# Four gate chunks move from the attention filler to a sixth Strassen group of the projections

## The chip, the cores and the metric

The kernel runs on one core of one Trainium2 chip. The metric is the device time of one execution in microseconds; the median of several runs is compared.

## What is computed

One layer of a bidirectional encoder: 1024 tokens of width 1024, all in float32. The reference, cut to what matters here:

```python
h = x + 0.5 * swiglu(rms_norm(x, n1), ...)            # feed-forward, d_ff = 2816
u = rms_norm(h, nm)
z = u @ w_in                                          # 1024 x 4352, one combined projection
qa, ka, va, qb, kb, vb, ga, gb = split(z)             # 3 x 512, 512, 2 x 128, 1024, 1024 columns
ya = neighbourhood_attention_2d(qa, ka, va, rpb)      # branch A: 8 heads of 64
yb = windowed_gqa_sink(rope(qb), rope(kb), vb, sink)  # branch B: 8 heads, 2 key/value heads
merged = sigmoid(ga) * (ya @ w_branch_a) + sigmoid(gb) * (yb @ w_branch_b)
h = h + merged @ w_out
h = h + 0.5 * swiglu(rms_norm(h, n2), ...)
y = rms_norm(h, nf)
```

## The kernel before, in words

Every large product is taken in three terms of 32-bit "high" and "low" parts: an operand is copied to a rounded high part (ScalarE) and the rest is subtracted out as a low part (VectorE, in places GpSimd), and `mm3` (L145, L147, L149) issues high x high, high x low and low x high, each a matmul with 128 x 512 output.

The order on every engine after the first stage is made by a planner: it takes the program in the order in which Python traced it as a priority, has costs of its own for each instruction, and issues what is ready by those costs. The order on each engine is then fixed. PSUM has two pools of four banks, called "d" and "g" in the names of the tiles.

The stages, in order of time, are: the first feed-forward (Strassen products, first its up, then its down part); the projections; attention, in which other products fill TensorE; the branch products; the product with `w_out`; and the second feed-forward.

**Projections.** The 34 chunks of 128 columns of `w_in` are numbered 0 to 33: 0 to 17 are queries, keys and values; 18 to 25 are the gates `ga` and 26 to 33 the gates `gb`. The list `groups` (L875) names chunks that are taken four at a time as a Strassen group: seven products (P1 to P7) for each of two pairs, `products` (L233 on) makes their operands (L308 on ScalarE, L311 and L315 on VectorE), and `store_z` (L879) evicts them and writes them to DRAM by GpSimd's queue. Hooks (L1030 on) place rotations, loads and reorderings of the other steps at fixed places before the end of this stage, and those at its start move with the number of groups.

**Attention.** `units_b` and then `units_a` give 64 units, 32 for each branch. For a unit, `scores` (L1278, L1279) issues the matmuls of two heads into two "d" banks, VectorE adds bias and takes the maximum (L1283), ScalarE takes the exponential (L1286), VectorE the reciprocal (L1289), and both engines scale (L1290, L1291). `turn` transposes on TensorE (L1299) into two "d" banks and splits the result into high and low parts (L93, L94). `values` (L1313 or L1318) multiplies with the values into a "g" bank, and `write` adds the parts (L1252 to L1256 for branch A). In one round of the loop the scores of unit n, the turn of unit n-1 and the values of unit n-2 are traced.

**The filler.** Between these steps the loop pulls steps of six large matmuls (two banks, three terms) from a generator, `filler`:

- first a `gate` for each gate chunk that is in no group: eight steps; its weights are split 1024 columns wide (L93, L94), its two "g" banks are copied out by ScalarE (L1127), and a DMA writes them to `g_d` (L1128);
- then `branch_b`: eight chunks of four steps, `yb @ w_branch_b`. Each splits a weight of 512 columns, loads a chunk of `gb` from `g_d` into one of two "xs" buffers (L1178), takes its sigmoid on ScalarE (L1179), and multiplies two banks, "d" for even chunks and "g" for odd ones, with it on VectorE (L1197);
- last, three of four steps of two chunks of `ya @ w_branch_a` (`branch_a`).

How many steps are pulled for a unit is set by `rate`; what is left is drained right after the loop. Before the change the 14 gates have 112 steps, `nfill` is 150 and `rate` is 106/64.

After that the branch-A products run chunk by chunk with sigmoids of `ga` (L1393), and GpSimd's queue stores combinations for the `w_out` product, which is a Strassen product again (`Down`).

Of the kernel before, what the change touches and what calls it, by code (L numbers as in the profile page):

```python
# [36 lines left out]
def trunk_kernel(ctx, tc, x, xt, n1, wg1, wu1, wd1, nm, win, rpb, sink, wa, wb, wo,  # L37
# [834 lines left out]
    mix = {}  # L872


    groups = [[(12, 13), (14, 15)], [(16, 17), (0, 1)], [(4, 5), (8, 9)], [(2, 3), (6, 7)], [(10, 11), (18, 19)]]  # L875
    NG = len(groups)
    gates = [dc for dc in [*range(8, 16), *range(8)] if 18 + dc not in sum((p for g in groups for p in g), ())]

# [336 lines left out]
    nfill = len(gates) * 8 + 38  # L1215
# [103 lines left out]
        un["write"](o)  # L1319

    pipe = []
    rate = (nfill - 44) / 64.0
    spent = 3.0

    def filling(share):
# [231 lines left out]
```

## Time and profile before

| quantity | before |
|---|---|
| median of 3 runs | 1936.27 us (1935.07 to 1936.42) |
| profiled execution: span | 1934.8 us |
| profiled execution: its own time | not listed apart; its span lies 0.3 us below the fastest run |
| TensorE busy | 1922.2 us (99%) |
| VectorE busy | 1437.1 us (74%) |
| ScalarE busy | 943.6 us (49%) |
| GpSimd busy | 295.5 us (15%) |

In the rows of the profile PE is TensorE's matmuls, PEld its weight loads, DVE is VectorE, ACT ScalarE, POOL GpSimd, and SP the engine that issues most loads. A row of a stretch gives its start and end, its length, the busy time of each engine in it with the number of instructions, TensorE's granted clock and the share of the DMA engines. A row of a group gives line, engine, operation, output and inputs, shapes and count, then the sum of durations, the mean duration in ns, and the idle time ahead of them with what ended it. Matmuls overlap one another, so that the mean duration of one is not what it takes of TensorE's time. In the busy time of a stretch, overlapping instructions of an engine count once.

### The profile page before, as it was taken

The page shows a single profiled execution, that of the slowest core. Times are in us where ns is not written, and L with a number is a line of the kernel's source. Part 1 is how long each engine was busy: PE and PEld are TensorE (multiplying, and loading weights), DVE is VectorE, ACT ScalarE, POOL GpSimd, SP SyncE. Part 2 cuts the span into 40 slices and gives each one's busy share as a digit, 9 for nine tenths or more (in the row PEclk, how much of TensorE's full clock was granted, in tenths as well). Part 3 has the DMA queues.
Part 4 walks back from the last instruction along what each step waited for, and adds up shares of the span by engine and source line. Part 5 has one row for each costly group of instructions (what it writes and reads, how often), then busy time and mean ns, then how long its engine had stood idle before and what let it go on. Part 6 is the DMA issues. An engine that isn't in the chain of part 4 may idle for free.

```text
span 1934.8 us, 25499 instructions
## 1 busy us (share of the span) xinstructions
PE 1922.2 (99%) x8956; PEld 1603.1 (83%) x8956; DVE 1437.1 (74%) x2560; ACT 943.6 (49%) x1827; POOL 295.5 (15%) x432
## 2 busy tenths in 40 slices
PE   9999999999999999999999999999999999999998
PEld 7888888888888888888888888878888888888886
DVE  7987765668957788678888857889676566569864
ACT  6532333344446543477877862365333333344453
POOL 0011110013300112211122231010111001005210
PEclk9999999999999999999999999999999999999999
DMA  6344323286234478553458576533423323493341
GB/s 261 100 167 163 129 104 128 86 289 225 88 109 137 159 223 250 185 163 104 116 134 195 184 242 210 169 140 133 147 87 109 126 87 109 140 355 104 112 144 61
DMA packets 151745, 298.70 MB, mean 154 GB/s; under 512 B 14912, under 2 KB 64448, under 8 KB 151616
## 3 DMA queue, kind: packets, MB, share of 16 engines
q1 hardware_dynamic: 123072, 210.53, 33.6%
q0 software_dynamic: 27824, 85.48, 13.3%
q8 instruction: 71, 1.16, 0.3%
q10 hardware_dynamic: 720, 1.05, 0.1%
q14 instruction: 58, 0.48, 0.1%
HBM read 210.50 MB, written 88.27 MB: 154 GB/s over the span
## 4 chain that ended last, share of the span: by engine, by line
PE 88%; issue 7%; POOL 1%; DMA 1%; DVE 1%; ACT 1%; POOLq 0%; SPq 0%; ACTq 0%; DVEq 0%
PE g L149 16%; PE g L147 16%; PE g L145 16%; PE d L149 11%; PE d L147 11%; PE d L145 11%; PE d L1299 2%; PE g L1313 1%; PE g L1318 1%; PE d L1278 1%; PE d L1279 1%; POOL zs_d L889 1%; PE d L138 1%; POOL z_d L891 1%; DMA zr_d<-xs 0%
## 5 line engine op out<-in xcount | busy, mean ns | idle before, releaser
L145 PE MATMUL g<-ar,ws 128*128 128x512 f32 x1128 | 423.1, 395 | 0.6 <-ACT fa L911 0.6
L147 PE MATMUL g<-ar,ws 128*128 128x512 f32 x1128 | 417.2, 390 | 0.9 <-DVE ar L94 0.5
L149 PE MATMUL g<-ar,ws 128*128 128x512 f32 x1128 | 416.1, 390 | 0.2 <-DVE ws L311 0.2
L145 PE MATMUL d<-ar,ws 128*128 128x512 f32 x736 | 282.4, 391 | 0.3 <-ACT ar L810 0.2
L147 PE MATMUL d<-ar,ws 128*128 128x512 f32 x736 | 281.9, 390 | 0.3 <-DVE ar L812 0.3
L149 PE MATMUL d<-ar,ws 128*128 128x512 f32 x736 | 281.6, 390 | 0.5 <-DVE ws L311 0.5
L147 PEld LDWEIGHTS g<-ar,ws 128*128 128x128 f32 x1128 | 211.8, 188 | 46.2 <-DVE ar L94 1.0
L149 PEld LDWEIGHTS g<-ar,ws 128*128 128x128 f32 x1128 | 211.7, 188 | 45.5 <-DVE ws L311 0.7
L145 PEld LDWEIGHTS g<-ar,ws 128*128 128x128 f32 x1128 | 206.4, 188 | 37.8 <-ACT fa L911 1.0
L311 DVE TENSOR_TENSOR ws<-raw,ws 128x512 fp32r<-128x512 f32 x204 | 139.6, 690 | 99.6 <-ACT ws L308 98.8
L308 ACT CAST ws<-raw 128x512 fp32r<-128x512 f32 x204 | 125.1, 620 | 140.6 <-PE g L149 64.4
L145 PEld LDWEIGHTS d<-ar,ws 128*128 128x128 f32 x736 | 138.3, 188 | 29.7 <-ACT ar L810 0.6
L147 PEld LDWEIGHTS d<-ar,ws 128*128 128x128 f32 x736 | 138.4, 188 | 29.6 <-DVE ar L812 0.6
L149 PEld LDWEIGHTS d<-ar,ws 128*128 128x128 f32 x736 | 138.4, 188 | 29.4 <-DVE ws L311 0.7
L93 ACT CAST ws<-raw 128x512 fp32r<-128x512 f32 (+1 forms) x121 | 81.0, 669 | 144.0 <-PE d L149 61.8
L94 DVE TENSOR_TENSOR ws<-raw,ws 128x512 fp32r<-128x512 f32 (+1 forms) x119 | 93.7, 789 | 59.8 <-ACT ws L93 59.3
L414 POOL DMA_DIRECT2D hid<-fx x91 | 49.3, 542 | 431.5 <-DVE fx L474 304.9
L93 ACT CAST ar<-raw 128x512 fp32r<-128x512 f32 (+1 forms) x83 | 56.0, 679 | 94.8 <-PE g L147 55.0
L94 DVE TENSOR_TENSOR ws<-ar,ws 128x512 fp32r<-128x512 f32 x114 | 98.3, 867 | 3.8 <-ACT ws L93 3.7
L145 PE MATMUL g<-ws,ws 128*128 128x512 f32 x232 | 91.0, 392 | 0.0
L149 PE MATMUL g<-ws,ws 128*128 128x512 f32 x232 | 90.5, 390 | 0.0
L147 PE MATMUL g<-ws,ws 128*128 128x512 f32 x232 | 90.3, 389 | 0.0
(313 smaller groups left out, 3607.4 us busy)
## 6 DMA issues: line engine op xcount, KB each, us to landing
raw<-hid SPq DMA_DIRECT2D x70, 512.0 KB
hid<-fx POOLq DMA_DIRECT2D x91, 256.0 KB, 2.4
ar<-in_ffn_w_down_dram SPq DMA_DIRECT2D x32, 512.0 KB
raw<-in_ffn_w_up_dram SPq DMA_DIRECT2D x31, 512.0 KB
raw<-in_ffn_w_gate_dram SPq DMA_DIRECT2D x27, 512.0 KB
raw<-in_w_in_dram SPq DMA_DIRECT2D x27, 512.0 KB
hid<-fa POOLq DMA_DIRECT2D x51, 256.0 KB, 2.7
ar<-zs_d POOLq DMA_DIRECT2D x48, 256.0 KB, 5.3
```

The costliest lines, as they stand in the source:

```text
L93: nc.scalar.copy(dst_hi, src)
L94: (eng or nc.vector).tensor_tensor(dst_lo, src, f32v(dst_hi), op=ALU.subtract)
L138: nc.tensor.transpose(pt[:, c * P:(c + 1) * P], xs[:, (half * 4 + c) * P:(half * 4 + c + 1) * P], ident)
L145: nc.tensor.matmul(b, lhs[0], r[0], start=first, stop=False, **kw)
L147: nc.tensor.matmul(b, lhs[0], r[1], start=False, stop=False, **kw)
L149: nc.tensor.matmul(b, lhs[1], r[0], start=False, stop=last, **kw)
L308: nc.scalar.copy(w[0][:, :512], a)
L311: nc.vector.tensor_tensor(w[0][:, 512:], a, f32v(w[0][:, :512]), op=ALU.subtract)
L414: nc.gpsimd.dma_start(hid[PRODUCTS.index(p), i], src)
L889: nc.gpsimd.dma_start(d[ch * P:(ch + 1) * P, cols], t)
L891: nc.gpsimd.dma_start(z_d[ch * P:(ch + 1) * P, cols], c)
L1299: nc.tensor.transpose(pt[:, i * P:(i + 1) * P], un["pr"][s][:, i * P:(i + 1) * P], ident)
```

## The change

Chunks 20 to 23, which are the gate chunks 2 to 5 of `ga`, become a sixth Strassen group. `gates` is derived from `groups` and so has 10 chunks instead of 14, 80 steps instead of 112; `nfill` falls from 150 to 118. The number subtracted in `rate` falls by as much, and the rate stays 106/64: attention pulls as many steps as before, and where steps of the four gates stood there now stand those of `branch_b`.

```diff
-    groups = [[(12, 13), (14, 15)], [(16, 17), (0, 1)], [(4, 5), (8, 9)], [(2, 3), (6, 7)], [(10, 11), (18, 19)]]
+    groups = [[(12, 13), (14, 15)], [(16, 17), (0, 1)], [(4, 5), (8, 9)], [(2, 3), (6, 7)], [(10, 11), (18, 19)], [(20, 21), (22, 23)]]
     NG = len(groups)
     gates = [dc for dc in [*range(8, 16), *range(8)] if 18 + dc not in sum((p for g in groups for p in g), ())]
...
     nfill = len(gates) * 8 + 38
...
-    rate = (nfill - 44) / 64.0
+    rate = (nfill - 12) / 64.0
     spent = 3.0
```

## The prediction

> **What bounds the kernel now.** I read the head of the page first, then the busy time by stretches, then in the stretch that the change touches the groups and the waits of each engine.
>
> ```profile
> span 1934.8 us, 25499 instructions
> PE 1922.2 (99%) x8956; PEld 1603.1 (83%) x8956; DVE 1437.1 (74%) x2560; ACT 943.6 (49%) x1827; POOL 295.5 (15%) x432
> L145 PE MATMUL g<-ar,ws 128*128 128x512 f32 x1128 | 423.1, 395 | 0.6 <-ACT fa L911 0.6
> ```
>
> TensorE is hardly ever without work, so at first sight whatever takes matmuls away is a gain. The third line shows a trap: 395 ns is how long one large matmul is under way, not what it takes. The price comes from a stretch of nothing but large matmuls, and beside it stand the stretches around the change:
>
> ```profile
> core 0: us, PE busy (x) PEld busy (x) DVE busy (x) ACT busy (x) POOL busy (x), PEclk, DMA share, GB/s
> 300.00:400.00 100.00, 100.00 (x443) 82.81 (x442) 64.18 (x98) 36.15 (x63) 10.85 (x20) 1.00 0.30 101
> 800.00:842.00 42.00, 42.00 (x187) 34.80 (x186) 26.86 (x42) 22.20 (x39) 6.84 (x13) 1.00 0.42 129
> 1034.00:1117.30 83.30, 83.30 (x498) 73.35 (x497) 73.07 (x231) 70.71 (x178) 19.46 (x24) 1.00 0.62 172
> 1126.00:1165.00 39.00, 39.00 (x173) 32.00 (x172) 17.18 (x26) 22.62 (x29) 9.46 (x9) 1.00 0.77 255
> ```
>
> 443 in 100 us is 0.2257 us for one. The 42 us before attention are the end of the projections, 1034 to 1117 the last third of attention, and 1126 to 1165 is where branch B's product runs now: there ScalarE has 16 us to spare and VectorE 22. In attention neither has much: ScalarE is idle for 83.3 - 70.7 = 12.6 us, VectorE for 10.2. TensorE sets the pace there only because the two others are just under it. ScalarE's work in that stretch:
>
> ```profile
> L1286 ACT ACTIVATE fa<-fa,nmx x40: 497/617/636, 1033.5 to 1116.8; 128x384 f32<-128x384 f32 x30, 128x256 f32<-128x256 f32 x10
> L1127 ACT COPY xs<-g 128x512 f32<-128x512 f32 x8 | 4.6, 596 | 0.3 <-PE g L149 0.2
> L93 ACT CAST ws<-raw 128x1024 fp32r<-128x1024 f32 x4 | 4.2, 1053 | 0.0
> ACT fa L1286 <- DVE nmx L1283: 6.2, 11, 1.2
> ```
>
> Forty exponentials are the last 20 units. The L1127 and L93 rows are the gates' share. The last row is who kept ScalarE waiting: the maximum from VectorE, 6.2 us of the 12.6.
>
> **Matmuls.** A gate is 8 steps of 6 large matmuls, four gates 192. A Strassen group is 7 products x 2 x 4 x 3 = 168. Nothing else on TensorE changes in number, and in the order in which the two programs stand, each has 672 filler matmuls between the first scores and the last values. So 24 x 0.2257 = **5.4 us** less for TensorE.
>
> **The sixth group.** It adds 37.9 us of matmuls at the projections. Its side work:
>
> ```profile
> L308 ACT CAST ws<-raw 128x512 fp32r<-128x512 f32 x204 | 125.1, 620 | 140.6 <-PE g L149 64.4 <-PE d L149 54.5 <-issue 18.2
> L311 DVE TENSOR_TENSOR ws<-raw,ws 128x512 fp32r<-128x512 f32 x204 | 139.6, 690 | 99.6 <-ACT ws L308 98.8
> L315 DVE TENSOR_TENSOR raw<-raw,raw 128x512 f32<-128x512 f32 x37 | 25.5, 688 | 0.7
> L911 ACT ACTIVATE fa<-g 128x512 f32<-128x512 f32 x24 | 14.4, 598 | 22.2 <-PE g L149 21.9 <-DVE fx L215 0.4
> L913 DVE SCALAR_TENSOR_TENSOR fa<-d,fa 128x512 f32<-128x512 f32 x16 | 10.9, 686 | 4.0 <-PE d L149 3.8
> ```
>
> ScalarE: 14 x 0.62 + 8 x 0.60 = 13.5 us. VectorE: 14 x 0.69 + 8 x 0.69 + 6 x 0.69 = 19.3 us. Both lie under 37.9 us of matmuls; at the end of the projections the engines are at about that share already (26.9 and 22.2 of 42) with TensorE at 42.0 of 42. Gate chunks need no high and low parts on eviction, and the rotations come no later against the start while the end moves away by a group. I take 0, bounds 0 and +1.
>
> **What takes the gates' place.** The order of the changed program says where branch B's product lands: its first sigmoid stands between the exponentials of the 18th- and the 17th-last unit, and between there and the last exponentials ScalarE has eight sigmoids (seven of branch B's, L1179, and one of L1393), each alone among exponentials. Before, all sigmoids follow attention. The two functions do not share a table:
>
> ```profile
> 1129.38 1.05 ACT L93 CAST ar<-fa 128x1024 fp32r<-128x1024 f32 x1
> 1130.45 1.28 ACT L1179 ACT_TABLE_LOAD   x1
> 1131.74 1.06 ACT L1179 ACTIVATE xs<-xs 128x1024 f32<-128x1024 f32 x1
> ...
> 844.24 1.28 ACT L1286 ACT_TABLE_LOAD   x1
> 847.09 0.51 ACT L1286 ACTIVATE fa<-fa,nmx 128x257 f32<-128x257 f32 x1 [1.56 <-DVE nmx L1283]
> ```
>
> The load begins when the copy ends, the sigmoid when the load ends: it holds the queue for its 1.28 us. The changed program has 20 loads where the old one has 4, sixteen more, all inside attention: to the sigmoid and back, eight times. Sum for ScalarE over the last 20 units, from these rows and this one,
>
> ```profile
> L93 ACT CAST ws<-raw 128x512 fp32r<-128x512 f32 x8 | 4.9, 618 | 3.4 <-DMA raw<-in_w_branch_b_dram 2.9 <-PE d L149 0.2 <-DMA raw<-in_w_branch_a_dram 0.2
> L1179 ACT ACTIVATE xs<-xs 128x1024 f32<-128x1024 f32 x8 | 8.5, 1061 | 10.8 <-DMA xs<-g_d 10.7
> ```
>
> is: added 16 x 1.283 = 20.5, 8 x 1.061 = 8.5 and 7 weight copies x 0.618 = 4.3; removed 6 gate copies x 0.596 = 3.6 and 4 wide weight copies x 1.053 = 4.2. Net **+25.5 us** on an engine with 12.6 to spare: 70.7 + 25.5 = 96.2 us of work where the stretch takes 83.3. With ScalarE never idle that stretch grows by 12.9 us; if all of its idle time stays, since it comes from waits inside a unit, by 25.5. I take half of the idle time as staying: the waits on VectorE's maximum are about half of it, and a ScalarE that runs late finds those maxima ready more often. That is 96.2 + 6.3 - 83.3 = **+19.2 us**.
>
> The Trainium skill speaks against the change here: "ScalarE: Activation LUTs", What ACT_TABLE_LOAD costs, puts a switch at about 1283 ns for the load and 1380 ns more for a drain, 2.66 us. The load agrees with the rows. The row at 1130.45 shows no drain before or after it. By the page, as an estimate, sixteen switches would take 42.6 us and the kernel about 1972 us.
>
> VectorE, by the order, gains fourteen products with the sigmoid, seven narrow low parts and one of the splits of branch B's output, and loses four wide ones:
>
> ```profile
> L1197 DVE TENSOR_TENSOR ar<-d,xs 128x512 f32<-128x512 f32 x8 | 5.2, 686 | 9.6 <-PE d L149 8.3 <-ACT xs L1179 1.1
> L94 DVE TENSOR_TENSOR ws<-raw,ws 128x1024 fp32r<-128x1024 f32 x4 | 4.9, 1220 | 0.8 <-ACT ws L93 0.8
> ```
>
> 14 x 0.686 + 7 x 0.69 + 1.2 - 4 x 1.22 = +10.8 us on 73.1: 83.9 us, a full engine at the old pace, but less than ScalarE's 96.2, so it adds nothing of its own.
>
> Who waits: in ScalarE's queue a pair of loads and a sigmoid, 3.6 us, stand ahead of the next unit's exponentials; behind those wait VectorE's reciprocal, both scalings, and TensorE's transposes, and TensorE issues in order, so the filler matmuls behind the transposes wait too. Even chunks of branch B also hold two of the four "d" banks that scores and turns need. The order shows it: filler matmuls per unit, a steady 12, 12, 6 before, become 22, 2, 0, 18, 10, 20, 0, 0, 18, 10, 14, 6, 0, 24, 4, 14 in the units before the last.
>
> ```profile
> L145 PE MATMUL g<-ar,ws 128*128 128x512 f32 x66 | 22.4, 417 | 0.0
> ```
>
> With 3 x 66 filler matmuls in the 20 units, a unit without filler is (83.3 - 198 x 0.2257) / 20 = 1.9 us for TensorE; ScalarE has no unit that short.
>
> **Behind attention.** 43.3 us of branch B's matmuls stand there no more; that is a shift, in the sum already. They were cover: for the last unit's write and split, and for loads.
>
> ```profile
> L1252 ACT COPY s<-g 64x256 f32<-64x256 f32 x19 | 7.0, 371 | 1.6 <-PE g L1313 1.1
> L1253 DVE TENSOR_TENSOR s<-g,s 64x256 f32<-64x256 f32 x19 | 7.8, 411 | 0.5 <-ACT s L1252 0.3
> L1256 DVE TENSOR_TENSOR fa<-g,s 64x128 f32<-64x128 f32 x40 | 11.2, 281 | 0.3
> L94 DVE TENSOR_TENSOR ar<-fa,ar 128x1024 fp32r<-128x1024 f32 x1 | 1.2, 1226 | 0.3 <-ACT ar L93 0.3
> ar<-in_w_out_dram SPq DMA_DIRECT2D x8, 512.0 KB
> 1166.27 6.27 SPq L537 DMA_DIRECT2D ar<-in_w_out_dram  x8
> ```
>
> Write and split take 0.37 + 0.41 + 2 x 0.28 + 1.05 + 1.23 = 3.6 us, and 36 matmuls, 8.1 us, are left over them. The loads of `w_out`, issued from 1166 on, are 4.2 MB, 16 us at the 255 GB/s of that stretch's row; their buffers now come free before attention ends, and 43 us of branch A's matmuls still lie ahead of their use. I take 0, bounds 0 and +3.6.
>
> **Sum.** The profiled execution's span is 1934.8; the median lies 1.5 us above it, which I carry along. 1934.8 - 5.4 + 19.2 = 1948.6, with the 1.5 **1950 us**. With ScalarE never idle it is 1944, with all its idle time kept 1956: that is the likeliest case's own range.
>
> **Rivals.**
>
> *The loads cost nothing* (the other side). Were the table loads hidden behind other work of ScalarE, its added work would be 25.5 - 20.5 = 5.0 us, less than the 12.6 to spare; TensorE would stay full and the 5.4 us come through: 1930.9. It decides if a load costs less than (12.6 - 5.0)/16 = 0.48 us. For it: the planner put the bursts of 18 to 24 matmuls where ScalarE's extra work is. Against it: 1.28 us, back to back, in both loads shown. 5%. A result within 3.9 us of the old time would need the stretch to grow by 1.5 to 9.3, below the floor of 12.9: 3%.
>
> *Sigmoids that wait for their data.* The sigmoid's input comes by DMA from `g_d`, and ScalarE issues in order. Before, ScalarE waited 10.7 us, seven times, for these loads (the L1179 row), which harmed nothing. Within attention 1.5 us for each of eight would stand before exponentials: +12, 1962. Against it: there the DMA share was 0.77, in attention it is 0.62. 14%.
>
> *A slower clock.* TensorE, never idle for long before, stalls some 2.4 us at each sigmoid.
>
> ```profile
> 1930.00:1934.80 4.80, 0.00 (x0) 0.00 (x0) 0.75 (x1) 0.72 (x1) 0.01 (x1) 0.59 0.29 109
> ```
>
> Without matmuls the granted clock falls to 0.59 within these 4.8 us; in every stretch above it is 1.00. If each of eight stalls cost as much as such a stretch, 4.8 x 0.41 = 2.0 us, it would be 16 us more, 1966. Against it: the stalls are half as long. 5%. The Trainium skill, "TensorE: Matmul & The Clock Gate", What's actually happening, has the clock halved after an idle window of about 3.4 us; by that rule stalls of this length mostly escape.
>
> *A switch that takes longer than its row.* At 844 the first exponential starts 1.56 us after its load has ended, put down to VectorE's maximum. If that were the switch itself, sixteen would add 25 us: 1975. Against it: the sigmoid at 1131.74 follows at once. 4%; the page cited above is the one that would have it so.
>
> That the planner would not put branch B into attention is no rival: the built order has it there.
>
> **How the numbers follow.** Forecast 69%, data waits 14%, clock 5%, longer switch 4%, no change 3%, loads hidden 5%. About 0.2% (3.9 us) is what a measurement of this kernel can tell from no change: faster 5%, the same 3%, slower 92%. The range 1942 to 1965 takes in the floor of ScalarE's sum with some margin and the data waits; it leaves out the hidden loads, the longer switch and part of the rest.
>
> **What would show it.** Right: 24 fewer large matmuls in all, with 672 of filler still within attention; sixteen more ACT_TABLE_LOAD of 1283 ns there; the last 20 units at about 102 us with ScalarE near 94% and idle TensorE put down to L1290, L1291 or L93; everything before attention's last third 38 us later and otherwise as before. Wrong: TensorE full through attention, or loads that overlap other ScalarE work; then the kernel is faster. If ScalarE's own idle time ahead of L1179 grows, it is the data.

## The result, and the profile after

The changed kernel takes **1972.55 us** (median of 5 runs, 1970.35 to 1974.03) where the kernel before took 1936.42 in the same comparison (1935.07 to 1937.06): ratio 1.0188, 95% interval 1.0177 to 1.0199. It is slower by 36 us, where 14 were forecast. The profiled execution is the slowest of the five (1974.03 us), so the stages of its trace differ by a little more, 37.4 us in all.

The head of the page after, and the busy time by stretches of the kernel after; the last stretch runs from the first scores of the 18th-last unit to the last values product of attention. The row of the kernel before for the same steps stands behind it.

```profile
span 1972.3 us, 25518 instructions
...
PE 1932.3 (98%) x8932; PEld 1605.2 (81%) x8932; DVE 1451.1 (74%) x2584; ACT 966.6 (49%) x1853; POOL 297.7 (15%) x436
```

```profile
300.00:400.00 100.00, 100.00 (x443) 82.81 (x442) 64.18 (x98) 36.14 (x63) 10.85 (x20) 1.00 0.29 103
838.00:880.00 42.00, 42.00 (x187) 34.75 (x187) 24.79 (x37) 21.79 (x36) 5.43 (x10) 1.00 0.35 110
1081.60:1205.80 124.20, 97.86 (x493) 79.92 (x493) 82.90 (x245) 99.27 (x202) 22.00 (x24) 0.88 0.53 148
```

```profile
1041.90:1124.90 83.00, 83.00 (x494) 73.01 (x493) 70.84 (x222) 70.39 (x173) 23.85 (x26) 1.00 0.65 179
```

24 matmuls fewer, as many in 100 us as before, TensorE still full at the end of the projections: those parts came as written down. The whole difference lies in the end of attention, where about the same number of matmuls takes 124.2 us instead of 83.0. By stages, in us:

| stage | before | after | difference |
|---|---|---|---|
| up to the first scores | 841.9 | 880.4 | +38.5 |
| units 0 to 45 | 200.0 | 201.1 | +1.1 |
| units 46 to 63 and the last turn and values | 83.0 | 124.2 | +41.2 |
| behind attention | 809.9 | 766.5 | -43.4 |

The 41.2 can be read from ScalarE's side. Its work in that stretch grew by 99.27 - 70.39 = 28.9 us. Its idle time grew from 12.6 to 24.9, and one wait accounts for 10.2 of that. The waits of ScalarE and of TensorE in the kernel after, each with the instruction that waits and the one waited for, the sum, the number of times and the longest:

```profile
ACT L1179 <- DMA xs<-g_d: 10.2, 1, 10.2
ACT s L1252 <- PE g L1313: 6.2, 5, 2.8
ACT fa L1286 <- DVE nmx L1283: 2.9, 3, 1.6
```

```profile
PE d L1299 <- DVE fa L1290: 17.3, 4, 11.4
PE g L1313 <- DVE ws L94: 4.0, 4, 1.8
```

The timeline shows that the longest wait of the one and the longest of the other are one event. Each row has the start, the duration, engine, line and operation, and in brackets the idle time before it:

```profile
1088.83 0.58 POOL L1128 DMA_DIRECT2D g_d<-xs  x1 [1.89 <-ACT xs L1127]
1089.07 1.28 ACT L1179 ACT_TABLE_LOAD   x1
1090.37 1.06 ACT L1179 ACTIVATE xs<-xs 128x1024 f32<-128x1024 f32 x1
1091.45 1.28 ACT L1286 ACT_TABLE_LOAD   x1
1092.74 0.51 ACT L1286 ACTIVATE fa<-fa,nmx 128x256 f32<-128x256 f32 x1
...
1093.67 0.32 SPq L1178 DMA_DIRECT2D xs<-g_d  x1
...
1105.57 1.28 ACT L1179 ACT_TABLE_LOAD   x1 [10.20 <-DMA xs<-g_d]
1106.86 1.06 ACT L1179 ACTIVATE xs<-xs 128x1024 f32<-128x1024 f32 x1
1107.93 1.28 ACT L1286 ACT_TABLE_LOAD   x1
1109.23 0.51 ACT L1286 ACTIVATE fa<-fa,nmx 128x256 f32<-128x256 f32 x1
...
1110.96 1.18 PE L1299 MATMUL d<-ident,fa 128*128 128x128 f32 x4 [11.35 <-DVE fa L1290]
```

The second sigmoid's data was asked for at 1093.67 and not there before 1105.5. It was not asked for earlier because its buffer, one of the two "xs", held the last gate's output: the store of that (L1128) was issued at 1088.83 and took 4.8 us to land, until 1093.6. ScalarE issues in order, so the pair of loads, the sigmoid and the exponentials of the next unit stood behind it, VectorE's scaling (L1290) behind those, and TensorE's transposes and all filler behind that. TensorE is named as waiting for VectorE; the cause is a DMA two engines further back. The DMA issues between 1085 and 1112, with their sizes and the median time to landing, show beside what the load ran:

```profile
ar<-zs_d POOLq DMA_DIRECT2D x12, 256.0 KB, 13.0
xs<-g_d SPq DMA_DIRECT2D x2, 512.0 KB
raw<-in_w_branch_b_dram SPq DMA_DIRECT2D x3, 256.0 KB
g_d<-xs POOLq DMA_DIRECT2D x1, 512.0 KB, 4.8
```

The twelve are the operands of the last head pair (L1090, L1092), which run at this place before, too.

From TensorE's side the 41.2 are three things: 26.3 us idle (124.20 - 97.86; before 0), a clock that is halved at times, and a rest of 5 us. These are stretches of the kernel after:

```profile
1085.00:1101.60 16.60, 12.52 (x60) 9.69 (x58) 12.68 (x38) 10.03 (x20) 8.06 (x15) 0.90 1.00 223
1101.60:1118.60 17.00, 6.82 (x20) 5.41 (x21) 5.00 (x17) 12.50 (x25) 0.00 (x0) 0.50 0.85 177
1118.60:1142.50 23.90, 20.97 (x121) 17.01 (x119) 19.89 (x60) 19.09 (x44) 0.58 (x1) 1.00 0.23 75
```

Five such pieces in attention's end have the clock at half, where before there is none; TensorE is busy for 19.9 us in them, so half of that, 9.9 us, is the halving.

### The profile page after: what moved, and what is told of

Same layout as the page of the kernel before. It is cut to its first block, busy times and chain, and to the rows that moved or that the text cites. A ratio compares the mean times of both kernels' runs of the same rounds, so it can differ in the third digit from the quotient of the medians.

```text
span 1972.3 us, 25518 instructions
## 1 busy us (share of the span) xinstructions
PE 1932.3 (98%) x8932; PEld 1605.2 (81%) x8932; DVE 1451.1 (74%) x2584; ACT 966.6 (49%) x1853; POOL 297.7 (15%) x436
## 4 chain that ended last, share of the span: by engine, by line
PE 80%; issue 9%; ACT 4%; DVE 3%; DMA 2%; POOL 2%; POOLq 0%; SPq 0%; DVEq 0%; ACTq 0%
PE g L145 15%; PE g L149 15%; PE g L147 15%; PE d L145 10%; PE d L149 10%; PE d L147 10%; PE d L1299 1%; PE g L1318 1%; ACT ws L93 1%; ACT fa L1286 1%; PE d L1278 1%; PE d L1279 1%; DMA ar<-zs_d 1%; POOL zs_d L889 1%; PE g L1313 1%
## 5 line engine op out<-in xcount | busy, mean ns | idle before, releaser
L145 PE MATMUL g<-ar,ws 128*128 128x512 f32 x1096 | 416.6, 396 | 3.5 <-ACT ws L93 2.8
L147 PE MATMUL g<-ar,ws 128*128 128x512 f32 x1096 | 411.1, 391 | 0.9 <-DVE ar L94 0.5
L149 PE MATMUL g<-ar,ws 128*128 128x512 f32 x1096 | 410.1, 391 | 0.2 <-DVE ws L311 0.2
L145 PE MATMUL d<-ar,ws 128*128 128x512 f32 x760 | 293.8, 393 | 0.8 <-ACT ws L308 0.4
L147 PE MATMUL d<-ar,ws 128*128 128x512 f32 x760 | 292.6, 392 | 0.6 <-DVE ar L812 0.6
L149 PE MATMUL d<-ar,ws 128*128 128x512 f32 x760 | 291.8, 391 | 0.5 <-DVE ws L311 0.5
L147 PEld LDWEIGHTS g<-ar,ws 128*128 128x128 f32 x1096 | 206.7, 189 | 44.9 <-DVE ar L94 1.0
L149 PEld LDWEIGHTS g<-ar,ws 128*128 128x128 f32 x1096 | 206.4, 188 | 44.3 <-DVE ws L311 0.7
L145 PEld LDWEIGHTS g<-ar,ws 128*128 128x128 f32 x1096 | 202.3, 189 | 42.6 <-ACT ws L93 4.0
L311 DVE TENSOR_TENSOR ws<-raw,ws 128x512 fp32r<-128x512 f32 x210 | 143.6, 689 | 107.6 <-ACT ws L308 106.7
L147 PEld LDWEIGHTS d<-ar,ws 128*128 128x128 f32 x760 | 143.5, 189 | 30.7 <-DVE ar L812 1.2
L145 PEld LDWEIGHTS d<-ar,ws 128*128 128x128 f32 x760 | 142.9, 189 | 31.1 <-ACT ws L93 1.0
L149 PEld LDWEIGHTS d<-ar,ws 128*128 128x128 f32 x760 | 143.2, 189 | 30.1 <-DVE ws L311 0.7
L93 ACT CAST ws<-raw 128x512 fp32r<-128x512 f32 (+1 forms) x117 | 76.7, 656 | 140.0 <-PE d L149 61.5
L94 DVE TENSOR_TENSOR ws<-raw,ws 128x512 fp32r<-128x512 f32 (+1 forms) x115 | 88.1, 766 | 56.3 <-ACT ws L93 55.8
L93 ACT CAST ar<-raw 128x512 fp32r<-128x512 f32 (+1 forms) x83 | 56.2, 679 | 92.0 <-PE g L147 54.5
L145 PE MATMUL g<-ws,ws 128*128 128x512 f32 x232 | 91.0, 392 | 0.0
```

Source lines behind the costliest of these rows:

```text
L93: nc.scalar.copy(dst_hi, src)
L94: (eng or nc.vector).tensor_tensor(dst_lo, src, f32v(dst_hi), op=ALU.subtract)
L145: nc.tensor.matmul(b, lhs[0], r[0], start=first, stop=False, **kw)
L147: nc.tensor.matmul(b, lhs[0], r[1], start=False, stop=False, **kw)
L149: nc.tensor.matmul(b, lhs[1], r[0], start=False, stop=last, **kw)
L311: nc.vector.tensor_tensor(w[0][:, 512:], a, f32v(w[0][:, :512]), op=ALU.subtract)
```

## The experiments

Each edit is against the changed kernel unless another is named. Times are medians, with the ratio to the kernel before and its interval; every group of runs had the kernel before beside it, at 1936 us.

**No table switch**: both sigmoids are left out, and plain copies of the same size stand in their place.

```diff
-        nc.scalar.activation(rb, rb, AF.Sigmoid)
+        nc.scalar.activation(rb, rb, AF.Copy)
...
-        nc.scalar.activation(r, r, AF.Sigmoid)
+        nc.scalar.activation(r, r, AF.Copy)
```

> The changed kernel with both sigmoids of the gates (branch B's and branch A's) left out and a plain copy of the same size in their place: ScalarE reads the same data at the same price, but its table is never switched. Theory T (the sixteen table switches hold ScalarE's queue and are the bulk of the loss): the attention stretch loses 20.5 us of ScalarE work, the kernel falls to 1940 to 1950 us. Theory D (the bulk is the one wait of ScalarE for a chunk of the gates, and what TensorE's clock loses after it): the wait stays, since the copy needs the same data, and the kernel stays at 1960 to 1970 us.

1955.53 us (1.0104, 1.0089 to 1.0119): 17.0 us gone and 19 us still there. That lies between the two forecasts, so neither the switches nor the wait is the bulk alone. The wait for the gates' load stays, now as the largest of ScalarE's:

```profile
ACT xs L1179 <- DMA xs<-g_d: 13.6, 3, 7.3
```

**A later preparation of the last head pair**, meant to move its twelve loads away from the gate's.

```diff
-    preps = {0: 23, 1: 33, 2: 41, 3: 49}
+    preps = {0: 23, 1: 33, 2: 41, 3: 51}
```

> The changed kernel with the loads of the last pair of branch A's heads begun two units later (unit 51 instead of 49), so that they do not run beside the first loads of branch B's gates. Theory D: the wait of 10.2 us in ScalarE goes and with it the lost clock, 1957 to 1962 us. Theory T: sixteen switches stay, 1967 to 1973 us. If the loads merely collide with the next chunk's, ScalarE shows a wait of several us at a later sigmoid.

1975.28 us (1.0201, 1.0186 to 1.0216). A miss as a test: the planner issued the loads at 1085 to 1098 as before, since the place in the traced order is only a priority, and the wait was still 9.2 us.

**No load of branch B's gates** (L1178 is left out; the sigmoids read a constant tile).

```diff
-        nc.sync.dma_start(rb, g_d[D + dc * P:D + (dc + 1) * P, :])
-        nc.scalar.activation(rb, rb, AF.Sigmoid)
+        src = masks[:, :1024]
+        nc.scalar.activation(rb, src, AF.Sigmoid)
```

> The changed kernel without the loads of branch B's gates: the sigmoid reads a constant that lies in SBUF. The sixteen switches and the eight sigmoids stay, no sigmoid can wait for data. Theory D: 1955 to 1962 us, and no stall over 4 us on TensorE in attention. Theory T: 1965 to 1971 us. What is left above 1931 us (the old time less 5.4 us of matmuls) is then the price of ScalarE's added work alone, which the prediction put at 13 to 26 us.

1965.46 us (1.0152, 1.0137 to 1.0167): 7.1 us gone, where theory T had 1965 to 1971. The edit also moved the planner's order: the table is loaded 22 times here, not 20, a ninth pair within attention. Two loads are 2.6 us of ScalarE's work, so the gates' load may have cost up to that much more than 7.1. ScalarE is now the fullest engine of attention's end, with 101.9 us of work in 116.0 (its row stands in the next section), and the clock is still halved in three pieces (8.7 us by the same reckoning).

**Sixteen switches alone, in the kernel before**: a sigmoid over 128 x 2 elements in eight of the last eighteen units, its result unused.

```diff
+        if npair[0] in (47, 48, 51, 53, 56, 58, 61, 63): nc.scalar.activation(small("tick"), ssum, AF.Sigmoid)
```

> The kernel before, with a sigmoid of 128 x 2 elements on the softmax sums, whose result nobody uses, at eight of the last eighteen units of attention: sixteen table switches (20.5 us of ScalarE) and some 2 us of tiny sigmoids, without any other part of the change. ScalarE has 12.6 us to spare there. Theory T: 8 to 22 us slower than before, 1944 to 1958 us. Theory D: the switches are mostly hidden, 1936 to 1942 us.

1951.26 us (1.0078, 1.0061 to 1.0095): 15 us slower, within the 8 to 22 of theory T. By the stages of its trace, 5.7 us of that lie in attention's end and 10.3 behind it. With the gates as filler, ScalarE took up nearly all of its idle time (first row, attention's end with all sixteen loads):

```profile
1040.50:1129.20 88.70, 86.55 (x494) 71.53 (x492) 69.96 (x221) 87.02 (x192) 18.41 (x24) 1.00 0.60 165
1129.00:1144.00 15.00, 7.96 (x20) 5.70 (x20) 10.34 (x13) 11.48 (x16) 7.81 (x4) 0.66 0.83 282
```

87.0 of 88.7 is 98%. What came behind attention came at once (second row), where branch B's start now found ScalarE late: one stall of 5.4 us ahead of L145, waiting for L93, and a halved clock after it.

**A sigmoid without a switch, with earlier loads.** 0.5 (tanh(x/2) + 1) is the sigmoid; the factor goes into the product behind. The gates are loaded into six half-width buffers instead of two.

```diff
+        rb = [main.tile([P, 512], F32, tag="hs", bufs=6, name=nm_("rb")) for _ in range(2)]
+        for n in range(2): nc.sync.dma_start(rb[n], g_d[D + dc * P:D + (dc + 1) * P, n * 512:n * 512 + 512])
+        for n in range(2): nc.scalar.activation(rb[n], rb[n], AF.Tanh, scale=0.5)
...
-                nc.vector.tensor_tensor(merged(dc)[:, sl], bs[n], rb[:, sl], op=ALU.mult)
+                nc.vector.scalar_tensor_tensor(out=merged(dc)[:, sl], in0=rb[n], scalar=1.0, in1=bs[n], op0=ALU.add, op1=ALU.mult)
```

> The changed kernel with both sigmoids written as 0.5 (tanh(x/2) + 1), for tanh is expected to share a table with the exponential (no switch), and with branch B's gates loaded into six half-width buffers that are free in attention, so that a load need not wait for one of the two buffers in use and lies ahead of the loads of the last head pair. If switches and that data wait are two separate costs that add up (17 us less without the switches, 7 us less without the loads): 1946 to 1950 us. If the data wait was only in the shade of the switches or the other way round: 1953 to 1957 us. If nothing else was wrong with the change: 1931 to 1935 us.

1957.79 us (1.0109, 1.0092 to 1.0126), just above the middle one of the three forecasts. The table is loaded three times in all. The wait for data did not go; it moved to the fourth chunk, whose load was issued at 1098.1:

```profile
ACT rb L1179 <- DMA rb<-g_d: 10.4, 2, 9.7
```

**The same with the tanh taken where the gate leaves PSUM** (L1127, in place of the copy), so that ScalarE does nothing on branch B's gates and no exponential stands behind their load.

```diff
-            nc.scalar.copy(gt[:, n * 512:(n + 1) * 512], bs[n])
+            nc.scalar.activation(gt[:, n * 512:(n + 1) * 512], bs[n], AF.Tanh, scale=0.5)
```

> As the run before, but tanh is taken where the gates leave PSUM, in place of the copy there, so that the eight passes of ScalarE over branch B's gates inside attention go (8.5 us of ScalarE's work), and no step of ScalarE waits for a gate from DRAM. If ScalarE's work is still what binds the last third of attention: 4 to 9 us less than the run before. If VectorE's added products, the two PSUM banks or the order bind it: within 2 us of the run before.

1943.85 us (1.0037, 1.0024 to 1.005): 28.7 us gone, and 13.9 against the run before, more than the 4 to 9 that were expected. This computes the whole layer, and it is still 7 us slower than the kernel before. Its attention's end:

```profile
1080.90:1176.50 95.60, 88.91 (x493) 73.91 (x492) 82.96 (x246) 70.12 (x177) 23.07 (x25) 0.98 0.64 181
```

**The rate left to follow the gates**, so that branch B stays behind attention and attention gets fewer filler matmuls.

```diff
-    rate = (nfill - 12) / 64.0
+    rate = (nfill - 44) / 64.0
```

> The sixth group alone: attention pulls filler at 74/64 steps for a unit, only the ten remaining gates, and branch B's product follows attention as before. No table switch, no gate load inside attention. TensorE has 1.9 + 1.16 x 6 x 0.2257 = 3.5 us of work for a unit, VectorE and ScalarE some 3.3 and 3.0 by their busy shares without the gates. If attention can run at TensorE's pace then: 1931 to 1936 us. If a unit's own chain of waits is longer than that: 1 us for each of 64 units more, up to 1995 us.

1945.17 us (1.0044, 1.0029 to 1.0059), between TensorE's pace (1931 to 1936) and the 1 us more for each unit that the forecast allowed. Attention is shorter but not full. This is all of attention, first in this kernel, then in the one before:

```profile
881.00:1134.00 253.00, 243.69 (x1469) 209.85 (x1468) 231.37 (x775) 216.97 (x566) 52.54 (x77) 0.99 0.57 150
```

```profile
842.00:1125.00 283.00, 282.33 (x1666) 247.81 (x1665) 237.71 (x779) 229.12 (x580) 55.99 (x82) 1.00 0.56 150
```

197 matmuls left it, 44 us by their price, and it became 30 us shorter: 14 us are lost here too, without any of branch B's work in attention.

**A rate between the two, with the tanh at eviction** (118 - 28 = 90 steps in 64 units).

```diff
-    rate = (nfill - 12) / 64.0
+    rate = (nfill - 28) / 64.0
```

> The second run of this set with a rate of 90/64 instead of 106/64: attention pulls the ten gates and about four of branch B's eight chunks, the rest follows. If VectorE binds the end of attention, fewer of its added products stand there, and it is 2 to 6 us faster than the second run; if a unit is bound by its own waits, it is slower, since TensorE has less to do beside them.

1945.26 us (1.0043, 1.0028 to 1.0059): not told apart from the full rate (1943.85), so neither forecast is borne out.

**No loads and turns for the last head pair** (left out; its units use the third pair's operands).

```diff
-            qs, kd, kl, va = heads_a[hp]
+            qs, kd, kl, va = heads_a[min(hp, 2)]
...
-    preps = {0: 23, 1: 33, 2: 41, 3: 49}
+    preps = {0: 23, 1: 33, 2: 41}
```

> The changed kernel without the loads and the value turn of the last head pair of branch A: its units use the pair before it. The sixteen switches and the loads of branch B's gates stay. If ScalarE's wait of 10.2 us for a gate chunk comes from sharing the DMA engines with those twelve loads of 256 KB: the wait falls under 2 us, and the kernel to 1957 to 1963 us. If it comes from the buffer that is freed late, or from the queue: the wait stays at 6 us or more and the kernel over 1966 us.

1966.03 us (1.0158, 1.0143 to 1.0174). The load is issued at the same moment as in the changed kernel (1093.63 against 1093.67), and ScalarE's wait for it falls from 10.2 to 3.3 us, so the twelve loads made most of it.

```profile
1093.63 0.34 SPq L1178 DMA_DIRECT2D xs<-g_d  x1
```

```profile
ACT L1179 <- DMA xs<-g_d: 3.3, 1, 3.3
```

The forecast had the wait under 2 us and the kernel at 1957 to 1963: the cause was right, the size was not. The time falls by 6.5 us, with work of the last pair left out too.

**VectorE relieved**, in two steps on the kernel with the tanh at eviction: first the low parts of branch B's weights on GpSimd, then the addition of mask and bias as well.

```diff
-                nxt = branch_w(wb[0], dc + 1, nc.vector), gate_b(dc + 1)
+                nxt = branch_w(wb[0], dc + 1, nc.gpsimd), gate_b(dc + 1)
...
-            nc.vector.tensor_tensor(bias_slot(s)[:, e, :].rearrange("p (d r w) -> p d r w", d=3, r=ROWS),
+            nc.gpsimd.tensor_tensor(bias_slot(s)[:, e, :].rearrange("p (d r w) -> p d r w", d=3, r=ROWS),
```

> The tanh-at-eviction version (1943.9 us), with the low parts of branch B's weights on GpSimd instead of VectorE, which takes some 5 us of VectorE's work from the last third of attention. If VectorE's added work is what is left of the loss there: 3 to 6 us less, 1938 to 1941 us. If the units' own waits are: within 2 us of 1943.9.

> As the run before, with the additions of mask and bias (sixteen, four for each head pair) on GpSimd too: another 4 us of VectorE's work out of that stretch. If VectorE binds: 1934 to 1938 us, about the time before or just under it. If GpSimd, slower at these operations, holds up the first units of a head pair: 1942 us or more.

1947.16 us (1.006, 1.0048 to 1.0073) and 1949.66 us (1.0069, 1.0057 to 1.0082): no gain from either, and the second is slower than the 1943.85 it started from, clear of the intervals. In the first, VectorE's busy time in attention's end fell from 82.96 to 78.90 us, and the stretch grew from 95.6 to 98.5:

```profile
1080.30:1178.80 98.50, 88.89 (x493) 73.82 (x493) 78.90 (x237) 70.36 (x177) 34.98 (x34) 0.98 0.62 178
```

So VectorE's fill is not shown to hold what was left. GpSimd is another engine with durations of its own, so this doesn't exclude it either.

**Both prices gone at once**: the copies instead of sigmoids and a constant tile instead of the load (both left out), the rest as in the changed kernel.

```diff
-        nc.sync.dma_start(rb, g_d[D + dc * P:D + (dc + 1) * P, :])
-        nc.scalar.activation(rb, rb, AF.Sigmoid)
+        src = masks[:, :1024]
+        nc.scalar.activation(rb, src, AF.Copy, scale=1e-30)
...
-        nc.scalar.activation(r, r, AF.Sigmoid)
+        nc.scalar.activation(r, r, AF.Copy)
```

> The changed kernel with both prices taken away at once: both gate sigmoids are plain copies (left out: the sigmoid, so no table switch) and branch B's copies read a constant tile (left out: the load of branch B's gates). Alone, the first took 17.0 us away and the second 7.1. If the two are separate prices, about 24 us go: 1946 to 1950. If they cover one another (a late load was hidden behind a switch), less: 1952 to 1956. If together they break the stalls that halve the clock, more: 1938 to 1944.

1944.15 us (1.0047, 1.0034 to 1.0059): 28.4 us gone, 4.3 more than the 24.1 of the two alone. The ninth pair of table loads in the run without the load can be 2.6 us of that, and the rest is no more than the intervals allow; so the two prices are separate as far as these runs can tell. That is the square of four from which the sizes below are read.

**The shared banks**: branch B's sums only in the "g" pool, first on the kernel with the tanh at eviction, then on the changed kernel itself.

```diff
-            bs = [bank("dg"[dc % 2]) for _ in range(2)]
+            bs = [bank("g") for _ in range(2)]
```

> e6 (tanh taken at the gates' eviction) with branch B's sums only in the two g banks, never in the d banks that scores and turns share. If the banks hold what is left of the loss at attention's end, some 7 to 10 us of the remaining 13 go: 1934 to 1938. If what is left is ScalarE and VectorE being nearly full, within 2 us of e6: 1942 to 1946; if two banks are too few for branch B, slower: 1947 and more.

> The changed kernel itself with branch B's sums only in the two g banks. If the d banks held by even chunks are what stalls it, 10 us or more go: under 1963. If the switches, the gate's load and the clock are the cause, as I hold, it stays within 3 us: 1969 to 1976.

1941.68 us (1.0032, 1.0019 to 1.0044) and 1969.66 us (1.0172, 1.0155 to 1.0189): 2 to 3 us each, inside the intervals. The banks are no large part.

No kernel here beats the one before.

## Why the prediction was wrong in size

The direction held, and so did the sums of the engines' work. The step that failed is the length of attention's end: ScalarE's work plus half of its idle time, +19.2 us, which made 102.5 us for the last 20 units with ScalarE 94% busy. From the scores of the 20th-last unit to the last scores the changed kernel takes 119.4 us with ScalarE 78% busy:

```profile
1070.70:1190.10 119.40, 96.24 (x496) 78.81 (x495) 83.92 (x247) 93.05 (x198) 23.46 (x23) 0.89 0.54 150
```

The sum had put two things at nothing: the wait for the gates' load, and what branch B's work as filler costs beside ScalarE's table switches. Both show in attention's end (bounded as in the table of stages) of the four kernels of the square: no switch and no load; no switch; no load; the rows of before and after stand further up.

```profile
1079.70:1175.20 95.50, 87.66 (x493) 72.98 (x492) 83.22 (x246) 76.91 (x184) 23.12 (x25) 1.00 0.56 153
```

```profile
1082.70:1190.60 107.90, 89.26 (x494) 74.19 (x493) 83.23 (x246) 77.04 (x184) 23.09 (x25) 0.95 0.60 170
```

```profile
1080.90:1196.90 116.00, 97.25 (x494) 78.91 (x493) 82.64 (x246) 101.85 (x203) 23.85 (x25) 0.91 0.48 134
```

| kernel | attention's end | longer than before by | TensorE idle | lost to the halved clock | kernel |
|---|---|---|---|---|---|
| before | 83.0 | | 0 | 0 | 1936.4 |
| neither switch nor load | 95.5 | 12.5 | 7.8 | 0 | 1944.2 |
| load, no switch | 107.9 | 24.9 | 18.6 | 1.7 | 1955.5 |
| switch, no load | 116.0 | 33.0 | 18.8 | 8.7 | 1965.5 |
| after | 124.2 | 41.2 | 26.3 | 9.9 | 1972.6 |

By the prediction's own steps:

- **24 matmuls less, 5.4 us.** Held: 8956 became 8932. The sixth group's 168 matmuls are 37.9 us by the same price, and the first scores came 38.5 us later; what it costs besides is 0.6, within the bounds of 0 and 1.
- **Behind attention, 0.** Held: 43.4 us shorter for 43.3 us of matmuls.
- **Sixteen loads at 1.28 us, nothing beside them.** Held: 20 loads in all, 1283 ns each, each starting as the instruction ahead of it ends.
- **ScalarE's work, +25.5 us.** Held in the stretch for which it was summed, so far as it can be compared: 93.05 us of work from the scores of the 20th-last unit to the last scores, where 96.2 were forecast, and the eighth pair, 3.6 us, just starts at the end of that stretch. VectorE's 83.9 came too (83.92).
- **"I take half of the idle time as staying."** This failed, in two ways. ScalarE was idle for 12.6 us of attention's end before and for 24.9 after. Take the wait for data away and 14.7 stay: all of the old idle time and 2 us more, the ceiling of the forecast and not its middle. The switches on the old filler (87.0 of 88.7 us busy) show that this idle time can be used nearly whole; with branch B as filler it wasn't.
- **"It adds nothing of its own"** for the rest of branch B's work, said of VectorE. This failed. With neither switch nor load, ScalarE has 76.9 us of work in 95.5 and VectorE 83.2, neither is the bound, and the stretch is still 12.5 us longer and the kernel 1944.2 - (1936.4 - 5.4) = 13.2 us above where the matmuls alone would put it. I took the busiest engine's sum as the length, and here no engine is full. All but 0.1 of TensorE's 7.8 us of idle time end with VectorE (4.7) or ScalarE (3.0), none with a DMA; the three largest stand behind this list. With 6.8 us less of ScalarE's work (the tanh at eviction) the stretch is as long, 95.6, and with 4.1 less of VectorE's it is 98.5. That the engines wait for one another in turn, which makes the stretch longer than the work of the fullest, fits this; it isn't shown by a run of its own.
- **The data wait as a rival (14%, +12).** It came, and not instead of the forecast but on top of it: +11.4 us without switches (1955.5 - 1944.2), +7.1 with them, where the kernel without the load has a pair of switches more. I had thought of 1.5 us at each of eight sigmoids; it was one wait of 10.2 us at the second, where the last head pair's twelve loads run. The DMA share of 0.62 that I held against it was a mean over 83 us; around this load it is 1.00 and 0.85 (the rows at 1085 and 1101.6).
- **The slower clock as a rival (5%, +16).** It came as well, in part: 9.9 us of TensorE's time. What of it reaches the end isn't shown, since no run sets the clock; where TensorE waits for ScalarE anyway, a slower TensorE would cost less than that.
- **A switch that takes longer than its row (4%, 1975).** The forecast from this rival is near the time measured, and it is still wrong: the exponential at 1109.23 starts 1.3 us after the start of its load, so nothing follows the load. By "ScalarE: Activation LUTs" of the Trainium skill, What ACT_TABLE_LOAD costs, there would be a drain of 1380 ns as well; no row here shows it.

TensorE's largest waits in attention's end with neither switch nor load:

```profile
PE d L145 <- DVE nmx L1283: 2.1, 2, 1.8
PE g L145 <- ACT ws L93: 2.1, 3, 1.2
PE g L1313 <- DVE ws L94: 1.9, 2, 1.7
```

Put together: with neither switch nor load 13.2 us are left, the switches on top of that are 1965.5 - 1944.2 = 21.3, and the load on top of both is 7.1. These three make up the whole because they are differences of one row of runs. The 21.3 stand against the 19.2 of the forecast, all of which hung on the switches (without them its 5.0 us of added work fit into 12.6); some of them come through the clock and the ninth pair. The other two were not in it: 2.1 + 13.2 + 7.1 = 22.4, and the forecast was 22.6 short. Taken away in the other order the load is 11.4 and the switches 17.0, so those two sizes are known to about 4 us. That switches and load cost this much is shown by leaving them out; the 13.2 are what remains, and their cause isn't shown.

"Wrong if ScalarE's own idle time ahead of L1179 grows, it is the data" was the right line to watch: the groups of before had 10.7 us there in the stretch behind attention, where it cost nothing, and the kernel after has 10.2 within attention.

**What stays open** is what holds these 13 us, the cost of the filler's composition. 7.8 are idle time of TensorE at a dozen places, the largest 1.7 and 1.8 us, ahead of L1313 and L145; the other 4.7 lie within matmuls' busy time. Neither the shared banks nor work moved from VectorE to GpSimd took a measurable part of it away. The unsteady filler (0 to 24 matmuls for a unit of the changed kernel) is a candidate that wasn't tried by itself, since the planner makes the order. The run with the rate left to follow the gates has no branch B in attention and lies 14 us above the matmuls' sum as well (1945.2 against 1931.0); whether the two losses have one cause is open too.

## What to carry to other kernels

When cheap work that fills an engine is exchanged for other work at the same rate, price what the new filler asks of the engines in the loop's chain, and add the prices: a switch, a load and a changed mix are not alternatives among which the likeliest counts. Read the DMA share at the moment at which an in-order engine will wait for a load, not over the stage, and keep an instruction that waits for DMA out of a queue on which the loop depends (taking the tanh where the gate leaves PSUM, with six buffers for the loads, removed switch and wait and gave back 28.7 of the 36 us lost). A function that shares the table of its neighbours is worth a little algebra.

## What the runs showed of the hardware

The clock is halved after shorter stalls than I had assumed. In the kernel after, the first piece of attention at half clock is 3.4 us long and begins at 1087.9, half a microsecond after a stall of only 1.75 us:

```profile
1087.39 0.39 PE L1313 MATMUL g<-ws,fx 128*128 128x256 f32 x1 [1.75 <-DVE ws L94]
```

```profile
1087.90:1091.30 3.40, 3.23 (x10) 2.42 (x10) 3.35 (x12) 3.35 (x5) 2.47 (x5) 0.50 0.90 185
```

A stall of the same length doesn't always do it. In the kernel without switch and load the same step leaves TensorE 1.73 us idle, and the clock stays at 1.00:

```profile
1082.00:1086.00 4.00, 2.27 (x19) 2.00 (x17) 3.66 (x10) 3.73 (x10) 2.91 (x3) 1.00 0.29 90
1086.00:1090.00 4.00, 3.54 (x20) 2.78 (x19) 3.76 (x14) 3.98 (x11) 3.04 (x6) 1.00 0.88 240
```

"TensorE: Matmul & The Clock Gate" of the Trainium skill, What's actually happening, gives a free-running window of 3413 ns. The length of the pieces agrees (3.4 us, or multiples); that an idle window of this length comes before the halving does not.

The tanh needs no load beside exponentials: the kernels with tanh have 3 loads in all, where the kernel before has 4.
